# Weight gradient on one core: whole result stores, halved first loads, and another order of visits

## The chip, the cores and the metric

The kernel runs on one core of a Trainium2 chip. The metric is the time of one execution on the device in microseconds (us); less is better. Five engines work side by side and meet only through semaphores: TensorE (PE in the profile; PEld is its loading of weights), VectorE (DVE), ScalarE (ACT), GpSimd (POOL) and SyncE (SP, which here only issues DMAs). A set of 16 DMA engines moves data between the chip's main memory (HBM) and the core's on-chip memory (SBUF). TensorE writes its results to PSUM, which has eight banks.

## The reference

```
batch, m, k, n = 16, 512, 1024, 768
input        float32 [16, 512, 1024]      # X
grad_output  float32 [16, 512,  768]      # G
grad_weight = einsum('bmk,bmn->kn', input, grad_output)     # float32 [1024, 768]
```

Batch and m are summed over together: the result is X^T G, with X of 8192 x 1024 and G of 8192 x 768. The inputs are read once (58.7 MB), the result of 3.1 MB is written once.

## The kernel before

**Slices and pairs.** The 8192 rows are cut into 64 slices of 128 rows, and two slices make a load `u` from 0 to 31 (line 12, `LOADS`). Loads 0 to 3 and 31 are multiplied directly, slice by slice (kind `s`). Loads 4 to 30 are pairs (kind `P`): there the kernel uses a seven-product scheme for 2 x 2 blocks. The two slices of a pair and the two halves of X's and G's columns form the blocks, and sums and differences of blocks (`xe`, `ge`, made on VectorE by `sum_x` and `sum_g`, lines 193 to 211, three instructions each) let seven products do what eight would.

**Streams, blocks, visits.** Products are named by letters and digits. A, B, C and D are the four quarters of the result (A: left half of X's columns with the left half of G's; B: left with right; C: right with left; D: right with right); 1, 5, 6 and 7 are the products of pairs that more than one quarter needs. Each stream has four blocks, `q` = 0 to 3, of 128 x 384 numbers. One visit multiplies one slice, or one product of a pair, into one block: a weight load of 128 x 128 and a matmul over 384 columns. There are 916 visits. A block's partial sum stands in a PSUM bank while it is open; it is closed into SBUF (`acc` for A to D, `macc` for 1, 5, 6, 7) and opened again later, so that the eight banks serve 32 blocks.

**The order.** `PLAN` (line 15) is a string of tokens that a search outside the kernel has found; the loop at line 396 turns each into instructions, in this order on every engine. `C0@6.1` is one visit of block C0, opened in bank 6; `C0.2` two more visits. `cC0` closes a block by a copy on ACT, `vC0` by a copy or an addition on VectorE. `fC0@4` fills bank 4 with the block's sum again (ACT). `zcD1.22` sets a sum aside into a buffer of its own (ACT; `zv` on VectorE), and `yD1.22` adds it back (VectorE). `wC1` adds a shared product into a block on POOL. `x1.9` and `g1.9` are the steps that make the sums of pair 9. `r11` is one of twelve roundings of slices 0 and 1 from float32 to bf16 (lines 218 to 231). A visit can begin when its data has landed (and been summed or rounded), and when its bank has been closed and, if wanted, filled.

**Loads.** Slices 0 and 1 of X and slice 0 of G come as float32 through SP and ACT (lines 143 to 146), four DMAs in all. Everything else comes through POOL, which casts to bf16 on the way (lines 162 to 180): from load 3 on one DMA of 384 KB for G and one of 512 KB for X of each pair. POOL issues a load when a buffer and a place in its queue are free; ten pairs can be held.

**The end.** The last close of A to D adds the shared product, and `store` (lines 333 to 341) sends the block to HBM through SP. Its first six DMAs are halves of 64 rows (`HALVED = 3` blocks, line 99); the later ones are whole blocks of 128 rows and 192 KB. The last block, B3, lies in two banks (`fB3@3+4`): its 256-column part is copied by ACT and stored through ACT, its 128-column part by VectorE and SP.

Of the kernel before, what the change touches and what calls it, by code (L numbers as in the profile page):

```python
# [9 lines left out]
P = 128  # L10
# [5 lines left out]
    "r11 r10 r16 r15 r14 r13 C0@6.1 r12 C1@4.1 vC0 C2@7.1 A0.1 cC1 A2.1 C3@5.1 cC2 r0 A1.1 A3.1 cC3 D3@4.1 "  # L16
    "B3@6.1 r4 r1 B2@3.1 B1@7.1 r2 r3 D1@5.1 vD3 D1.1 A3.1 A2.1 cD1 B3.1 B2.1 B1.1 B0@4.1 cB2 B0.1 vB1 A1.1 "
    "cB3 D2@5.2 vB0 fC3@3 C0@7.1 A0.1 C2@6.1 cD2 C2.1 D0@4.2 vC2 D0.1 D2@5.1 C3.1 B2@6.1 vD2 A3.1 cC3 C0.1 "
    "A2.1 vD0 D1@5.1 B1@3.1 A0.2 C0.1 D1.1 A3.1 vC0 A1.1 zcD1.22 A1.1 C1@4.1 vB2 C1.2 C3@5.2 D3@6.4 C1.1 A3.1 "
    "vD3 A1.1 B1.2 vC3 B0@6.3 D0@7.2 vB0 D2@5.3 C1.1 B1.1 vD2 D3@6.1 A1.1 D0.1 vD3 A3.1 B2@5.2 vB1 B2.1 "  # L20
    "D1@6.2 vB2 C2@3.3 yD1.22 A0.2 vC2 C0@5.2 A2.2 vD1 A2.1 B3@3.1 vC1 B3.3 vC0 B3.2 A3.1 D0.1 vB3 D0.1 "
    "D3@5.2 vD0 fB1@3 B0@6.3 vD3 A2.2 vB0 D1@7.1 fC2@5 D1.1 D2@4.2 fC1@6 A0.2 vD2 B1.2 C1.1 g0.4 fC3@4 C1.1 "
    "A1.2 vD1 cB1 C2.2 g1.4 A3.1 C0@7.1 C3.1 g2.4 C3.3 x0.4 C3.1 C1.1 A2.1 cC3 C2.1 x1.4 C0.2 cC2 13@4.1 x2.4 "
    "B2@3.1 cC1 A3.1 vC0 A0.1 c13 B1@5.1 61@6.1 B2.1 vB1 B2.1 c61 B0@4.1 A1.1 vB2 B3@5.1 12@7.1 71@6.1 vB3 "
    "10@3.1 g0.5 11@5.1 vB0 11.1 x0.5 10.1 12.1 c11 13@4.1 A3.1 c12 A1.1 v13 50@5.1 c10 50.1 71.1 x1.5 A0.1 "
    "c50 73@7.1 g1.5 73.1 c71 g0.6 A2.1 51@3.1 c73 51.1 g2.5 61@4.1 53@5.1 c51 53.1 v61 60@7.2 c53 70@6.1 "
    "g1.6 70.1 fC0@4 52@3.1 g2.6 52.1 72@5.1 x2.5 72.1 c52 C0.1 x0.6 C0.1 A2.1 63@3.1 cC0 63.1 x1.6 70.1 72.1 "
    "73@4.1 c70 x2.6 60.1 A3.1 c72 v73 63.1 B0@6.1 c60 B0.1 g0.7 B3@5.2 fC1@7 B2@4.1 vB0 B2.1 A1.1 c63 A0.1 "
    "vB3 C1.1 62@6.2 g1.7 62.1 vB2 C2@5.2 c62 C1.1 g2.7 13@3.1 f51@4 13.1 x0.7 A1.1 C1.1 fC0@6 A2.1 v13 51.1 "
    "cC1 51.1 C2.1 x1.7 A3.1 c51 C0.1 vC2 11@3.2 cC0 A0.1 71@7.1 v11 fC3@4 71.1 53@6.2 f50@5 g0.8 C3.2 f52@3 "  # L30
    "v53 C3.1 50.2 g1.8 52.2 x2.7 12@6.2 g2.8 x0.8 12.1 A2.1 A3.1 zc12.3 A1.1 C3.1 x1.8 52.1 50.1 cC3 71.1 "
    "x2.8 73@6.1 c52 73.1 v71 72@4.1 c50 72.1 61@3.1 v73 61.1 fB1@5 61.1 v72 A0.1 63@6.1 fB2@7 63.1 v61 B1.2 "
    "f10@4 B1.1 v63 B1.1 B2.2 cB1 g0.9 10.2 f60@6 10.1 x0.9 10.1 B0@3.1 cB2 B0.1 A0.1 g1.9 c10 51@5.1 x1.9 "
    "51.1 f62@7 60.1 g2.9 60.2 x2.9 C2@4.2 c60 v51 62.3 y12.3 B3@6.2 c62 B3.1 vC2 A1.1 f53@5 B0.1 A3.1 vB3 "
    "70@7.1 f13@4 70.2 g0.10 zcB0.0 11@6.2 13.1 g1.10 f52@3 13.2 x0.10 11.1 A1.1 c13 A3.1 52.1 x1.10 52.1 "
    "fC1@4 53.1 g2.10 53.1 c52 53.1 v11 70.1 A2.1 c53 A2.1 x2.10 A0.1 f73@3 C0@6.1 v70 C0.2 fB2@5 C1.1 g0.11 "
    "C1.1 fC3@7 C1.1 73.1 vC0 73.1 cC1 B2.1 yB0.0 B2.1 f71@6 C3.2 72@4.1 x0.11 71.1 cC3 A3.1 A1.1 cB2 71.1 "
    "x1.11 71.1 f63@7 73.1 g1.11 72.2 c71 x2.11 61@5.2 v72 c73 61.1 63.2 g2.11 63.1 fB0@4 B1@3.1 v61 B1.1 "
    "f60@6 B1.1 g0.12 B0.2 c63 A2.1 vB1 51@5.1 cB0 51.1 60.1 g1.12 60.1 12@7.2 g2.12 c60 12.1 x0.12 12.1 "
    "fB3@3 A1.1 C2@6.2 fC1@4 v12 C2.1 51.1 B3.1 x1.12 f53@7 B3.1 C1.1 v51 A2.1 cB3 A0.1 53.1 g0.13 53.1 f50@3 "  # L40
    "C1.1 52@5.1 vC2 52.1 cC1 50.1 x2.12 50.2 f13@4 v52 50.1 C3@6.1 c53 C3.1 g1.13 A3.1 A0.1 fC0@5 vC3 13.2 "
    "c50 13.1 x0.13 11@7.2 f72@3 11.1 70@6.1 g2.13 70.1 v11 70.1 C0.2 x1.13 C0.1 72.1 g0.14 72.1 cC0 62@7.2 "
    "c72 v70 62.2 fB2@5 A0.1 x2.13 A2.1 63@3.1 c13 v62 63.1 A1.1 B2.1 g1.14 B2.1 fC2@7 B2.1 v63 10@4.2 cB2 "
    "10.1 x0.14 10.2 A0.1 51@6.1 x1.14 51.1 71@3.1 g2.14 71.1 zc51.23 71.1 v10 C2.2 61@5.1 v71 61.1 cC2 61.1 "
    "x2.14 A2.1 fB0@6 72@3.1 v61 73@4.2 fB3@7 73.1 g0.15 B0.1 f13@5 B0.2 v73 A1.1 A3.1 cB0 A3.1 v72 B3.3 13.1 "
    "x0.15 13.1 cB3 11@4.2 c13 g1.15 52@6.2 v11 52.1 53@7.2 v52 53.1 f60@4 B1@3.2 x1.15 B1.1 fC1@6 60.1 v53 "
    "60.1 f12@5 60.2 g2.15 A3.1 vB1 C1.1 c60 C1.2 fC3@7 g0.16 A0.1 70@4.1 A2.1 f50@3 12.1 g1.16 12.2 x0.16 "
    "12.1 50.2 c12 x2.15 50.2 cC1 g2.16 C3.2 v70 c50 C3.2 10@6.1 x1.16 10.1 cC3 A0.1 g0.17 A2.1 70@5.1 fC0@7 "
    "70.1 v10 A1.2 f71@3 A3.1 g1.17 62@6.1 v70 62.2 71.1 g2.17 71.1 C0.1 v62 C0.1 c71 C0.2 x0.17 A3.1 f61@3 "
    "A1.1 A2.1 cC0 C2@6.1 x1.17 C2.2 f73@5 x2.16 61.2 vC2 61.1 73.2 c61 x2.17 73.1 63@6.1 fB2@7 g0.18 63.3 "  # L50
    "fB1@3 y51.23 B0@4.2 c73 B0.1 g1.18 A0.1 B1.1 vB0 f72@5 B1.2 B2.1 g2.18 B2.1 cB1 B2.1 x0.18 B2.1 A0.1 "
    "A3.1 cB2 v63 51@4.3 x1.18 51.1 f63@6 72.2 x2.18 72.2 v51 52@3.3 g0.19 53@7.1 fB3@4 53.2 v52 63.1 B3.2 "
    "v53 c63 B3.2 g1.19 C1@3.2 cB3 C1.1 13@6.1 x0.19 13.1 f71@4 13.2 c72 A1.2 v13 71.3 vC1 f10@6 12@7.2 x1.19 "
    "12.1 f11@5 60@3.2 g0.20 c71 60.2 v12 11.3 v60 11.1 A0.1 A3.1 g1.20 70@7.1 f50@3 70.1 g2.19 70.1 g2.20 "
    "10.3 x0.20 10.1 50.2 c10 v70 50.2 A0.1 fB2@6 x2.19 A2.3 x1.20 c50 73@7.2 c11 x2.20 73.1 62@4.1 g0.21 "
    "fC3@3 62.3 B2.1 g1.21 B2.1 v73 B2.1 B1@5.2 cB2 v62 B1.1 C3.2 g2.21 C3.2 x0.21 C3.1 C2@7.2 cC3 C2.1 vB1 "
    "C2.1 A2.1 72@6.1 vC2 72.2 52@4.1 x1.21 52.2 g0.22 A3.2 61@3.1 v72 61.2 g1.22 61.1 51@7.2 v61 63@6.3 "
    "g2.22 f13@3 C0@5.1 v52 C0.3 v51 C0.1 fC1@4 13.2 x0.22 13.1 C1.2 c13 C1.1 x1.22 C1.1 zc63.13 A1.3 x2.21 "
    "fB0@6 x2.22 A0.2 B3@7.1 g0.23 cC1 B3.2 vC0 B3.1 51@3.2 vB3 B0.3 v51 B0.2 12@5.1 g1.23 12.1 cB0 12.1 "
    "x0.23 12.1 f72@7 A3.2 v12 A0.1 70@4.2 y63.13 70.2 A1.1 x1.23 72.2 v70 71@5.2 c72 71.1 g0.24 71.1 f10@6 "  # L60
    "53@3.2 g2.23 53.2 v71 53.1 A2.2 x2.23 11@4.1 v53 11.3 x0.24 11.1 A2.1 A3.1 50@5.2 x1.24 50.2 g1.24 "
    "62@7.1 v11 62.1 zc50.5 62.2 g0.25 51@3.1 f60@4 51.1 73@5.2 v51 73.2 60.1 g1.25 f61@3 60.1 v62 60.3 v73 "
    "61.1 fC2@7 61.2 c60 A0.1 x0.25 A0.1 10.1 fB2@5 10.2 x1.25 10.2 g2.25 63@4.2 c10 x2.24 63.2 x2.25 B2.2 "
    "g0.26 B2.3 v63 B1@6.2 cB2 B1.1 g1.26 B1.2 g2.26 B0@5.2 g2.24 B0.1 C3@4.1 vB1 C3.3 vB0 C3.1 C0@6.1 y50.5 "
    "C0.1 f52@5 C0.2 vC3 C2.1 c61 C2.2 x0.26 C2.2 60@4.1 A2.1 cC2 A2.1 x1.26 A3.1 f13@3 A3.1 x2.26 52.2 g0.27 "
    "52.3 v60 B3@7.2 c52 B3.1 vC0 B3.1 13.1 f52@4 13.1 g1.27 13.1 fB2@6 13.1 x0.27 13.1 12@5.2 c13 12.1 x1.27 "
    "12.1 52.1 73@3.1 v12 73.1 c52 73.1 A0.1 x2.27 A0.1 53@4.1 vB3 53.3 g0.28 50@5.2 v53 50.1 B2.2 g1.28 "
    "51@7.2 cB2 v50 A1.4 v51 A3.2 x0.28 f63@7 72@4.3 g2.28 72.2 x1.28 73.1 63.2 v73 63.1 70@6.2 g0.29 c63 "
    "70.2 fC3@3 g2.27 70.1 71@5.1 v72 71.1 f61@7 71.2 x2.28 71.1 C0@4.1 v70 C0.1 61.2 g1.29 61.2 vC0 C1@6.2 "
    "c61 g2.29 C1.2 x0.29 C1.1 f62@7 C1.2 C3.1 v71 C3.2 A1.1 x1.29 A1.1 cC3 62.1 vC1 62.3 g0.30 f71@6 62.1 "  # L70
    "11@3.1 x2.29 11.1 f12@5 11.1 g1.30 11.1 f10@4 11.1 A2.3 12.2 x0.30 12.1 10.2 c12 10.1 g2.30 10.2 x1.30 "
    "f61@5 11.1 71.1 c10 71.1 v11 62.1 61.2 f51@4 v62 13@3.3 v61 f60@7 51.2 x2.30 51.1 f72@5 51.1 60.1 v13 "
    "60.2 v71 60.2 72.2 v51 f63@6 wC1 A3.3 f73@3 A3.1 63.2 v60 A0.3 v72 fC1@7 A0.2 73.1 v63 f52@5 73.1 wC2 "
    "C1.2 fD1@4 v73 C1.1 52.2 cC1 52.1 A2.1 f53@6 A2.1 v52 A2.1 A1.1 f70@3 A1.2 fB2@7 D1.2 vA2 wD2 70.1 fC0@5 "
    "70.1 B2.2 v70 B2.3 vD1 fB1@3 C0.2 vA1 C0.1 fC2@4 C0.1 53.2 vC0 53.1 C2.2 vA3 fC3@5 C2.2 v53 C2.1 f50@2 "
    "C2.1 C3.2 cC2 C3.1 B1.2 vC3 fD3@6 wB3 B1.3 vA0 fB0@5 B1.2 vB2 50.1 fD2@4 50.2 vB1 D3.1 fD0@7 D3.1 D2.1 "
    "v50 D2.1 B0.2 cD2 B0.3 fB3@3+4 vD3 B0.2 D0.2 vB0 B3.4 vD0 B3.2 cB3 "
).split()


WARMUP = [("b", 512), ("f", 512), ("f", 512), ("b", 512)]
PAIRS_HELD = 10
SUMS_HELD = 8
ASIDE = 24

# [8 lines left out]
    2: [(1, 256, 0, 256), (2, 0, 256, 384)],  # L94
    3: [(2, 128, 0, 384)],
}


HALVED = 3


@with_exitstack
def kernel(
# [6 lines left out]
    nc = tc.nc  # L110
# [161 lines left out]
    stored = []  # L272
# [179 lines left out]
```

## Time and profile before

| | us |
|---|---|
| median of 3 runs (163.1 to 163.17) | 163.13 |
| the profiled execution's own time | 161.59 |
| its span, first to last instruction | 159.8 |
| TensorE busy | 154.8 (97% of the span) |
| VectorE busy | 143.7 (90%) |
| ScalarE busy | 96.4 (60%) |
| first matmul on data | 5.28 |
| last matmul ends | 155.86 |

The profile is one execution, and times in it count from its first instruction. The rows of the busy view have 40 slices of 4 us, each digit the busy share in tenths. A row of the timeline or of the chain begins with start and length in us; a bracket at its end tells how long the engine stood idle before and what ended that. `L323 MATMUL` are the visits, `L322` weight loads that are issued a second time, `L341` the stores. In the rows of the DMA issues the last number is the median time from issue to landing. Durations of neighbouring instructions of one engine overlap: VectorE's 128 x 384 additions take 551 ns each and start 468 ns apart when nothing waits.

### The profile page before, as it was taken

The page shows a single profiled execution, that of the slowest core. Times are in us where ns is not written, and L with a number is a line of the kernel's source. Part 1 is how long each engine was busy: PE and PEld are TensorE (multiplying, and loading weights), DVE is VectorE, ACT ScalarE, POOL GpSimd, SP SyncE. Part 2 cuts the span into 40 slices and gives each one's busy share as a digit, 9 for nine tenths or more (in the row PEclk, how much of TensorE's full clock was granted, in tenths as well). Part 3 has the DMA queues.
Part 4 walks back from the last instruction along what each step waited for, and adds up shares of the span by engine and source line. Part 5 has one row for each costly group of instructions (what it writes and reads, how often), then busy time and mean ns, then how long its engine had stood idle before and what let it go on. Part 6 is the DMA issues. An engine that isn't in the chain of part 4 may idle for free.

```text
span 159.8 us, 2985 instructions
## 1 busy us (share of the span) xinstructions
PE 154.8 (97%) x1002; PEld 99.1 (62%) x1129; DVE 143.7 (90%) x333; ACT 96.4 (60%) x219; POOL 39.7 (25%) x75
## 2 busy tenths in 40 slices
PE   8999999999999999999999999999999999999990
PEld 3466666567677777776665656666656666666560
DVE  0665989999999999999999999999999999898990
ACT  3761036588698999767868655254354525678750
POOL 7445222122221222221222221222222100024300
PEclk9999999999999999999999999999999999999998
DMA  5999999999999999999999999999999999931696
GB/s 176 298 209 212 216 212 212 213 213 215 210 212 213 213 214 212 213 213 215 213 213 214 212 214 211 213 215 209 214 214 213 215 211 214 212 73 28 172 366 226
DMA packets 12734, 33.41 MB, mean 209 GB/s; under 512 B 1456, under 2 KB 4528, under 8 KB 12720
## 3 DMA queue, kind: packets, MB, share of 16 engines
q0 software_dynamic: 9648, 28.64, 90.8%
q1 hardware_dynamic: 2640, 3.41, 6.7%
q10 hardware_dynamic: 432, 1.18, 1.9%
q8 instruction: 8, 0.13, 0.3%
q14 instruction: 6, 0.05, 0.1%
HBM read 58.72 MB, written 3.15 MB: 387 GB/s over the span
## 4 chain that ended last, share of the span: by engine, by line
PE 93%; DMA 3%; DVE 1%; ACT 0%; issue 0%; ACTq 0%
PE bank L323 93%; DMA xf<-in_input_dram 3%; DVE acc L366 1%; ACT xp L215 0%; ACT acc L362 0%; ACTq L362 0%
## 5 line engine op out<-in xcount | busy, mean ns | idle before, releaser
L323 PE MATMUL bank<-gp,xp 128*128 128x384 bf16 (+2 forms) x672 | 108.2, 307 | 0.3 <-DVE acc L366 0.2
L323 PEld LDWEIGHTS <-xp 128*128 128x128 bf16 x672 | 62.4, 97 | 31.4 <-DVE xp L215 1.7
L323 PE MATMUL bank<-ge,xe 128*128 128x384 bf16 x324 | 63.6, 326 | 0.0
L323 PEld LDWEIGHTS <-xe 128*128 128x128 bf16 x324 | 30.9, 97 | 15.4 <-DVE xe L197 0.4
L366 DVE TENSOR_TENSOR macc<-bank,macc 128x384 f32<-128x384 f32 x70 | 37.5, 551 | 0.6 <-PE bank L323 0.4
L362 ACT COPY macc<-bank 128x384 f32<-128x384 f32 x58 | 26.7, 482 | 13.5 <-PE bank L323 13.1
L294 ACT COPY bank<-macc 128x384 f32<-128x384 f32 x54 | 25.6, 484 | 9.0 <-DVE macc L366 5.7
L362 ACT COPY acc<-bank 128x384 f32<-128x384 f32 (+1 forms) x47 | 21.9, 477 | 14.6 <-PE bank L323 14.5
L294 ACT COPY bank<-acc 128x384 f32<-128x384 f32 (+1 forms) x48 | 22.6, 483 | 13.3 <-DVE acc L366 9.5
L366 DVE TENSOR_TENSOR acc<-bank,acc 128x384 f32<-128x384 f32 x51 | 26.8, 552 | 3.5 <-PE bank L323 2.9
L169 POOL DMA_DIRECT2D xp<-in_input_dram x29 | 15.3, 528 | 49.5 <-DMA xp<-in_input_dram 14.9
L168 POOL DMA_DIRECT2D gp<-in_grad_output_dram x29 | 15.3, 528 | 37.6 <-PE bank L323 20.4
L197 DVE TENSOR_TENSOR xe<-xp 128x1024 bf16<-128x1024 bf16 x27 | 18.5, 684 | 0.7 <-DMA xp<-in_input_dram 0.6
L207 DVE TENSOR_TENSOR ge<-gp 128x768 bf16<-128x768 bf16 x27 | 14.8, 550 | 0.0
L199 DVE TENSOR_TENSOR xe<-xe,xp 128x512 bf16<-128x512 bf16 x27 | 11.3, 420 | 0.4
L201 DVE TENSOR_TENSOR xp<-xp,xe 128x512 bf16<-128x512 bf16 x27 | 11.1, 419 | 0.2
L322 PEld LDWEIGHTS <-xp 128*128 128x128 bf16 x79 | 7.7, 98 | 4.6 <-DMA xp<-in_input_dram 0.4
L209 DVE TENSOR_TENSOR ge<-gp,ge 128x384 bf16<-128x384 bf16 x27 | 9.4, 350 | 0.1
L211 DVE TENSOR_TENSOR gp<-ge,gp 128x384 bf16<-128x384 bf16 x27 | 9.3, 351 | 0.1
L394 POOL TENSOR_TENSOR acc<-acc,macc 128x384 f32<-128x384 f32 x4 | 4.0, 1000 | 21.8 <-DVE macc L359 17.8
L378 ACT COPY aside<-bank 128x384 f32<-128x384 f32 x6 | 2.9, 480 | 6.0 <-PE bank L323 6.0
L322 PEld LDWEIGHTS <-xe 128*128 128x128 bf16 x48 | 4.7, 98 | 2.8 <-DVE xe L197 0.2
(23 smaller groups left out, 37.9 us busy)
## 6 DMA issues: line engine op xcount, KB each, us to landing
xp<-in_input_dram POOLq DMA_DIRECT2D x29, 512.0 KB, 16.8
gp<-in_grad_output_dram POOLq DMA_DIRECT2D x29, 384.0 KB, 16.8
out_dram<-acc SPq DMA_DIRECT2D x12, 192.0 KB, 2.2
xf<-in_input_dram ACTq DMA_DIRECT2D x2, 512.0 KB, 5.0
xp<-in_input_dram POOLq DMA_DIRECT2D x4, 256.0 KB, 8.5
gp<-in_grad_output_dram POOLq DMA_DIRECT2D x5, 192.0 KB, 7.7
out_dram<-acc SPq DMA_DIRECT2D x6, 96.0 KB, 2.2
gf<-in_grad_output_dram SPq DMA_DIRECT2D x2, 192.0 KB, 4.1
```

The source lines that it names most:

```text
L168: nc.gpsimd.dma_start(out=gp, in_=G[rows, :].rearrange("(p m) n -> p m n", m=2))
L169: nc.gpsimd.dma_start(out=xp, in_=X[rows, :].rearrange("(p m) k -> p m k", m=2))
L197: nc.vector.tensor_sub(out=xe[:, 0:2, :], in0=x[:, 1::-1, :], in1=x[:, 3::-2, :])
L199: nc.vector.tensor_sub(out=xe[:, 2, :], in0=xe[:, 0, :], in1=x[:, 0, :])
L201: nc.vector.tensor_add(out=x[:, 1, :], in0=x[:, 2, :], in1=xe[:, 2, :])
L207: nc.vector.tensor_add(out=ge[:, 0:2, :], in0=g[:, 0:2, :], in1=g[:, 1::2, :])
L209: nc.vector.tensor_add(out=ge[:, 2, :], in0=g[:, 3, :], in1=ge[:, 0, :])
L294: copy(out=tile_[:, t0 : t0 + c1 - c0], in_=sum_of(p, q)[:, c0:c1])
L322: nc.tensor.ldweights(stat)
L323: nc.tensor.matmul(tile_[:, t0 : t0 + c1 - c0], stat, mov[:, c0:c1], start=start, stop=True, skip_group_check=True,)
L362: nc.scalar.copy(out=d, in_=b)
L366: nc.vector.tensor_add(out=d, in0=b, in1=d)
```

## The change

Three things are changed. All result blocks are stored whole. X of slice 0 and G of slice 0 (each half of its columns) are loaded in two halves of 64 rows, in the same queues as before. And `PLAN` is replaced by another order that the search has found, for the same 916 visits.

```diff
-HALVED = 3
...
-    nc.sync.dma_start(out=gf[:, LEFT], in_=G[0:P, LEFT])
-    nc.scalar.dma_start(out=xf[0], in_=X[0:P, :])
-    nc.sync.dma_start(out=gf[:, RIGHT], in_=G[0:P, RIGHT])
+    HALVES = (slice(0, P // 2), slice(P // 2, P))
+    for rows in HALVES:
+        nc.sync.dma_start(out=gf[rows, LEFT], in_=G[0:P, LEFT][rows, :])
+        nc.scalar.dma_start(out=xf[0][rows, :], in_=X[0:P, :][rows, :])
+    for rows in HALVES:
+        nc.sync.dma_start(out=gf[rows, RIGHT], in_=G[0:P, RIGHT][rows, :])
     nc.scalar.dma_start(out=xf[1], in_=X[P : 2 * P, :])
...
-        halves = [slice(0, P)]
-        if len(stored) < 2 * HALVED:
-            halves = [slice(0, P // 2), slice(P // 2, P)]
-        for rows in halves:
-            stored.append(rows)
-            queue.dma_start(out=OUT[rows, row, at : at + c1 - c0], in_=sum_of(p, q)[rows, c0:c1])
+        queue.dma_start(out=OUT[:, row, at : at + c1 - c0], in_=sum_of(p, q)[:, c0:c1])
```

The order of visits, its beginning and its end:

```diff
-    "r11 r10 r16 r15 r14 r13 C0@6.1 r12 C1@4.1 vC0 C2@7.1 A0.1 cC1 A2.1 C3@5.1 cC2 r0 A1.1 A3.1 cC3 D3@4.1 "
-    "B3@6.1 r4 r1 B2@3.1 B1@7.1 r2 r3 D1@5.1 vD3 D1.1 A3.1 A2.1 cD1 B3.1 B2.1 B1.1 B0@4.1 cB2 B0.1 vB1 A1.1 "
+    "r11 r10 r16 r15 r12 r13 C0@4.1 r14 C3@3.1 r0 C2@5.1 A2.1 cC3 A1.1 vC2 A0.1 cC0 A3.1 D1@7.1 D0@6.1 B2@3.1 "
+    "D2@5.1 r4 r2 B1@4.1 vD1 cD0 B1.1 A0.1 r3 A3.1 vB1 B0@6.1 cD2 B0.1 B3@7.1 r1 B3.1 cB0 B2.1 A1.1 C1@4.1 "
...
-    "C2.1 C3.2 cC2 C3.1 B1.2 vC3 fD3@6 wB3 B1.3 vA0 fB0@5 B1.2 vB2 50.1 fD2@4 50.2 vB1 D3.1 fD0@7 D3.1 D2.1 "
-    "v50 D2.1 B0.2 cD2 B0.3 fB3@3+4 vD3 B0.2 D0.2 vB0 B3.4 vD0 B3.2 cB3 "
+    "cC1 wD2 B1.1 C0.1 vA2 C0.1 fB2@4 C0.3 vB1 fC2@6 50.2 fD2@7 vC0 50.1 B2.2 f53@5 v50 B2.2 fD3@3 D2.2 53.2 "
+    "cD2 vB2 53.1 D3.2 v53 C2.1 fC3@4 C2.2 fB0@7 C2.3 vA3 fD0@5 C2.1 wB3 C3.2 vD3 C3.1 D0.2 vC3 B0.3 vD0 "
+    "fB3@3+4 B0.2 vC2 B0.2 B3.2 vB0 B3.4 cB3 "
```

Counted over both strings: visits 916 and 916, fills 102 and 103, closes on ACT 105 and 102, closes on VectorE 150 and 144, sums set aside and added back 6 and 12, additions on POOL 4 and 3.

## The prediction

> **What bounds the kernel now.** I read the page's busy rows first, then the chain that ended last, then TensorE's weight loads for the waits behind it, then the stages of the DMA.
>
> ```profile
> PE   8999999999999999999999999999999999999990
> DVE  0665989999999999999999999999999999898990
> DMA  5999999999999999999999999999999999931696
> ```
>
> Three resources are full at once: TensorE, VectorE (90% of the span) and, until slice 35, the DMA engines. The chain says where one hands over to another:
>
> ```profile
> 0.73 4.12 DMA xf<-in_input_dram
> ...
> 5.29 22.56 PE bank L323 x153
> 27.85 0.02 issue
> 27.87 1.55 DVE acc L366 x3
> 29.42 0.04 issue
> 29.46 13.38 PE bank L323 x85
> 42.84 0.06 issue
> 42.90 112.86 PE bank L323 x746
> ```
>
> Columns are start, length, work. Work on data starts at 5.29 us, when X of slice 0 has landed (4.86) and been rounded; the last matmul ends at 155.86. The orders hold 916 visits; one visit is 384 columns and starts 162.5 ns after the one before it where nothing waits, so 149 us of the 150.6 are streaming, and gaps between matmul starts add to 1.3 us: 13 gaps, of which 1.13 us lie before 42.9 us and 0.19 us (four gaps) after. An order of visits can win at most those. The gaps before 42.9 end on loads:
>
> ```profile
> 20.66 1.41 PEld L323 LDWEIGHTS <-xp 128*128 128x128 bf16 x10 [0.26 <-DMA xp<-in_input_dram]
> ...
> 29.78 0.44 PEld L323 LDWEIGHTS <-xp 128*128 128x128 bf16 x4 [0.71 <-DMA xp<-in_input_dram]
> ...
> 42.85 0.10 PEld L322 LDWEIGHTS <-xp 128*128 128x128 bf16 x1 [0.40 <-DMA xp<-in_input_dram]
> ```
>
> Here TensorE stands still until X of pairs 3, 5 and 8 has landed (20.62, 29.74, 42.81). After that it stays 0.1 to 0.6 us behind nearly every landing. So the landing of pair 8 fixes the time of all that follows, and what shifts the load stream shifts the end. The stream itself, by stage (us, then busy time and count of each engine, clock, DMA share, GB/s):
>
> ```profile
> 1.75:2.75 1.00, 1.00 (x2) 0.33 (x1) 0.00 (x0) 1.00 (x1) 1.00 (x3) 1.00 0.89 204
> 2.75:4.25 1.50, 1.50 (x3) 0.48 (x2) 0.00 (x0) 0.19 (x1) 1.50 (x4) 1.00 0.99 395
> ...
> 43.00:139.00 96.00, 96.00 (x634) 63.38 (x736) 94.19 (x221) 61.66 (x141) 20.59 (x39) 1.00 1.07 213
> ...
> 149.00:151.00 2.00, 2.00 (x15) 1.21 (x13) 2.00 (x6) 1.54 (x4) 0.16 (x1) 1.00 0.66 158
> 152.00:156.00 4.00, 3.85 (x30) 2.50 (x28) 3.86 (x10) 2.13 (x6) 0.00 (x0) 1.00 1.02 367
> ```
>
> The engines fill up within a second microsecond and never go idle again until 139 us (213 GB/s counts the bf16 that lands; twice that is read). The last two rows are stores: in halves of 64 rows 158 GB/s, whole 367.
>
> **Part 1: three blocks stored whole instead of in halves.** Lines 333 to 341 no longer split the first three blocks: 17 stores in all where there were 20 (one of them ACT's in both). What it costs now:
>
> ```profile
> 148.97 1.80 SPq L341 DMA_DIRECT2D out_dram<-acc  x3
> ...
> 155.80 0.91 SPq L341 DMA_DIRECT2D out_dram<-acc  x2
> ...
> out_dram<-acc SPq DMA_DIRECT2D x4, 96.0 KB, 2.2
> ...
> out_dram<-acc SPq DMA_DIRECT2D x1, 64.0 KB, 2.6
> ```
>
> The first row is two halves and one whole store, 0.60 us each; later ones follow every 0.49 us. The halves put SP 0.87 us behind (the fourth block, A1, is closed at 149.37 and issued at 150.24); the queue stays full to 154, and a whole store needs 0.53 us of the engines (196.6 KB by 367 GB/s), so the arrears pass from SP to the engines: a store lands 2.05 us after its issue at 151.3 but 2.58 after it at 156.3. That last one lands at 158.90, and 0.91 us of closing work ends the span at 159.81. Without halves SP saves three issues of 0.6 us, all in the first 4 us of the tail, where nothing waits for it; what reaches the end is the arrears, at most 0.5 us.
>
> **Part 2: the end of the order.** The last 18 visits change. Before, VectorE closes D3, B0 and D0 from 154.27 to 155.75, and B3's two parts follow: SP is still busy with D0 until 156.21, so B3's narrow part, copied by 156.18, is issued at 156.32. After, D0 closes before C2 and B0; B0's last visit is 6 visits (0.98 us) before the end, so VectorE has closed it some 0.3 us before TensorE is done and SP is free. B3 now gets four visits in one step, so its wide part is complete four 128-column matmuls (0.21 us) before the end instead of two (0.11): ACT copies 0.1 us earlier. Counting back from the end, the last six blocks become ready 2.9, 2.4, 1.9, 1.4, 0.7 and 0.3 us before it, mean spacing 0.53, the engines' own pace, with a pause of 1.4 us ahead of them. Arrears go. The last issue moves from 0.45 to 0.35 us after the last matmul and its landing from 2.58 to 2.1 to 2.4. Parts 1 and 2 together: a gain of 0.2 to 0.6 us; I take **0.45**. The cover of ACT's store (issued 0.37 us after the last matmul, landing 2.50 later) moves the same way.
>
> **Part 3: slice 0 in halves.** SP issues four loads for two, ACT three for two; ACT's table load (1.66 us, 1.28 long) moves back by one issue of 0.41 and still ends a microsecond before the first rounding at 4.38. SP has nothing queued behind until the stores. A rounding now waits for two landings; the first half's is the earlier and costs nothing. X of slice 1 is issued 0.41 us later; its packets have no turn before 4.2 us anyway. What decides is how fast 64 rows load. The trace has no such load. Nearest row: stores of 64 rows, packets of the same 1536 bytes. From 147.5 to 151 us 406 packets took 59.9% of 16 engines, from 151 to 154.5 us 903 took 100.4%: 83 ns against 62, and with the 4-byte ones out (80 and 102) about 101 against 69. A half is not a whole at half length: each packet is slower.
>
> Bounds for the stream: at the good end, the half issue of G costs 0.19 us instead of 0.38 ahead of X, whose first packet follows G's by 0.38 us now: 0.2 us earlier. At the bad end halves with the same rows are always in flight together and go at half rate: of the 721 KB of X and G's left half, 204 pass in the slow first microsecond as now, and the other 517 need 2.5 us at 205 GB/s instead of 1.26: 1.2 us later. Between: G's packets run 0.38 us ahead, so its second half rides beside X's first. Then X alone sets the time, 524 KB at about 210, 2.5 us, with 197 KB of G beside it: 721 KB that full rate would pass in 1.76. Of the 0.74 lost, some 0.3 fall into the slow start that is there anyway. I take **0.4 us** later, since both queues start as now and alternate packet by packet. G of slice 1 and all pairs follow by as much, TensorE waits for them at pairs 5 and 8, and the end moves by all of it.
>
> In the Trainium skill, "SBUF — State Buffer", section "Door 1: The DMA port swizzle", 64 neighbouring partitions reach only 8 of 16 ports; the 158 against 367 GB/s agree. By its half rate alone the sum would be the bad end.
>
> **Part 4: the order of visits.** First uses of loads barely move: pair 5 at visit 146 in both, pair 8 at 224 in both, pair 14 at 384 instead of 385, pair 30 at 812 instead of 811. At the old landings no first use after pair 5 would come too early, so the order neither adds a load wait nor can win one. G of slice 1 is needed at visit 12 instead of 13: 0.16 us more waiting there, swallowed by the waits at pairs 5 and 8. VectorE's work: 111 adding closes for 121, but 12 sums set aside and added back for 6 (549 ns each), and 9 copies for 6: with one more final close and one sum set aside by VectorE itself that is one instruction more, 0.47 us of its 144. It is full from 30 us on; by visits its account differs from before's by 0 to 0.5 us either way (beyond a constant 0.47 from the first 16 visits, where it was idle). What of its backlog reaches TensorE was 0.19 us after 42.9; the bounds are 0 and some 0.7 (the gap of 0.33 at 28.98, when it closed three blocks in a row, twice over). I take 0.19 again: nothing.
>
> **Sum.** 0.4 later, 0.45 earlier, 0: minus 0.05 us on the profiled execution's 161.59 (span 159.8 and 1.8 around it). That execution is 1.5 us under the median of the three runs; the difference carries over: 163.13 - 0.05, **163.1 us**. Below 0.2% (0.33 us) a measurement here can't tell a change from none: I forecast no change.
>
> **Rivals.**
> *Halves load as fast as wholes.* Reads that wait for memory may hide the slower packets; the first row of stages (204 GB/s) shows engines waiting then. Against it, the stores. No cost, or 0.2 gained, less 0.45: 163.13 - 0.55, **162.6**. The Trainium skill's "Perfetto Trace Analysis", "DMA Optimizations", says smaller chunks may let some start sooner where engines are idle; no run here shows it.
> *Halves in step* (slower): X's and G's first halves go together, then the second halves, at the bad end of part 3. For it, alternating queues; against it, G's head start. The page on SBUF named above would have it so. 163.13 + 1.2 - 0.45, **163.9**. It decides from a delay of 0.8 us on.
> *VectorE late.* With no idle time between 30 and 140 us, a crowded stretch of closes holds banks back: 0.7 us after pair 8, **163.75**. For it, visits 820 to 880, where the new order asks 10.45 us of VectorE in 9.75; against it, 900 visits on which the accounts match.
> *The stores gain nothing,* since the last waits for its own close anyway: **163.5**. Against it, the growing landings.
>
> **Chances.** Forecast 0.36 (its own range 162.8 to 163.45), fast halves 0.28, in step 0.17, VectorE late 0.14, stores 0.05. Faster 0.28, same 0.36, slower 0.36. Range 162.4 (early start and the full 0.6) to 164.0 (in step with the smaller gain); below and above it I leave a tenth each.
>
> **What would show it.** Right: X of pair 8 lands 0.4 us after 42.81, the first matmul comes 0.05 to 0.5 us after 5.29, the last store lands 2.1 to 2.4 us after its issue, the span less the last matmul's end is 3.4 to 3.5 instead of 3.95, and gaps after pair 8 are near 0.2 us. Wrong: a first matmul before 5.2, pair 8 at or before 42.8, or VectorE releasing gaps of over 0.5 us late in the run.

## The result and the profile after

The change takes 167.2 us (median of 4 runs, 166.64 to 168.39) where the kernel before takes 163.12 beside it: a ratio of 1.028, interval 1.021 to 1.035. It is 4 us slower; forecast was no change, 163.1, in a range of 162.4 to 164.0.

The profiled execution of the change took 167.31 us, its span 165.5 (before 161.59 and 159.8). The busy view, 40 slices of 4.14 us:

```profile
PE   8199999999999999999999999999999999999991
...
DVE  0135698999999999999999999999999999889991
...
PEclk9957999999999999999999999999999999999999
DMA  4999999999999999999999999999999999300775
```

What differs lies in the first slices. TensorE stands nearly idle in the second, and its granted clock falls to 5 tenths and 7 tenths in the third and fourth; from the fifth on its row reads as before, VectorE's from the sixth, but for the shift at the end. The timeline of the change up to the first visit (start, length, what; the bracket is idle time and what ended it):

```profile
0.73 1.18 SPq L143 DMA_DIRECT2D gf<-in_grad_output_dram  x2
0.74 1.45 ACTq L144 DMA_DIRECT2D xf<-in_input_dram  x2
...
6.98 1.28 ACT L216 ACT_TABLE_LOAD   x1 [6.98 <-DMA gf<-in_grad_output_dram]
...
8.67 7.54 PE L323 MATMUL bank<-gp,xp 128*128 128x384 bf16 x30 [3.79 <-ACT gp L216]
```

The first visit begins at 8.67 us instead of 5.28. The chain that ended last says what it waited for. From there on TensorE runs to the end with hardly a break: the two closes on ACT at 39.9 us make one matmul start 0.29 us late.

```profile
1.33 5.57 DMA gf<-in_grad_output_dram
...
6.98 0.25 ACT L216
7.23 1.04 issue
8.27 0.36 ACT gp L216
...
8.67 31.20 PE bank L323 x191
39.87 0.02 issue
39.90 0.38 ACT macc L357
40.27 0.04 issue
40.31 0.49 ACT acc L357
40.80 0.04 issue
40.84 120.99 PE bank L323 x798
```

The second half of G's left part, issued at 1.33, lands at 6.91; only then does ACT load its table (1.28 us) and round. The DMA issues of the change, with KB each and the median us from issue to landing, stand against 5.0 us for X and 4.1 for G before:

```profile
xf<-in_input_dram ACTq DMA_DIRECT2D x2, 256.0 KB, 4.9
xf<-in_input_dram ACTq DMA_DIRECT2D x1, 512.0 KB, 8.1
gf<-in_grad_output_dram SPq DMA_DIRECT2D x4, 96.0 KB, 6.3
```

In the median, half the bytes take about as long or longer, and the whole load behind them (X of slice 1) takes 8.1. Single landings, from the trace:

| lands at, us | before | change (first, second half) |
|---|---|---|
| G of slice 0, left | 4.35 | 3.22, 6.91 |
| X of slice 0 | 4.86 | 4.60, 7.19 |
| G of slice 0, right | 5.67 | 9.06, 10.48 |
| X of slice 1 | 7.14 | 10.31 |
| G of slice 1 (POOL's first) | 7.49 | 7.14 |

One load became earlier: POOL's. The stages of the change (us, busy time and count of each engine, granted clock, DMA share, GB/s):

```profile
1.75:2.75 1.00, 1.00 (x2) 0.33 (x1) 0.00 (x0) 0.00 (x0) 1.00 (x3) 1.00 0.89 197
2.75:4.25 1.50, 1.50 (x3) 0.48 (x2) 0.00 (x0) 0.00 (x0) 1.50 (x4) 1.00 0.84 196
4.25:5.25 1.00, 0.64 (x2) 0.00 (x0) 0.00 (x0) 0.00 (x0) 1.00 (x3) 1.00 1.17 319
...
8.67:14.75 6.08, 6.08 (x22) 2.75 (x22) 2.27 (x6) 3.29 (x9) 2.61 (x5) 0.51 1.13 221
14.75:20.00 5.25, 5.25 (x40) 3.50 (x39) 3.82 (x8) 1.09 (x3) 2.05 (x5) 1.00 1.11 215
```

and two rows of the same view of the kernel before:

```profile
4.25:5.25 1.00, 0.95 (x2) 0.00 (x0) 0.66 (x3) 0.72 (x3) 1.00 (x3) 1.00 1.07 419
...
8.67:14.75 6.08, 6.08 (x42) 3.77 (x41) 3.74 (x8) 2.48 (x6) 3.00 (x6) 1.00 1.13 207
```

From 2.75 to 4.25 us the change moves 196 GB/s where 395 moved before. And from 8.67 to 14.75 TensorE is "busy" all the time in both, but does 22 matmuls against 42, at a clock of 0.51. A full busy row is not full speed; the count beside it shows that. Matmuls are not quite visits: 80 of the 916 visits go to a block that lies across two banks, and such a visit is two matmuls, over 256 and over 128 columns.

**Where the 5.7 us of span come from.** By 14.75 us the change has begun 20 visits and the kernel before 57 (counted in the trace's records, a split visit once). 37 visits of 0.1625 us are 6.0 us, and the last matmul ends 5.96 us later (161.81 against 155.85). So the whole loss has been made by 14.75 us; behind it the late starts of matmuls add to about 1 us in both kernels. The end gives 0.28 back: the span less the last matmul's end is 3.69 instead of 3.96.

### The profile page after: what moved, and what is told of

It is laid out like the page before. It is cut to its first block, busy times and chain, and to the rows that moved or that the text cites. A ratio compares the mean times of both kernels' runs of the same rounds, so it can differ in the third digit from the quotient of the medians.

```text
span 165.5 us, 3000 instructions
## 1 busy us (share of the span) xinstructions
PE 157.1 (95%) x1002; PEld 100.4 (61%) x1129; DVE 143.5 (87%) x334; ACT 97.0 (59%) x222; POOL 39.0 (24%) x74
## 4 chain that ended last, share of the span: by engine, by line
PE 92%; DMA 3%; ACT 1%; issue 1%; SPq 0%; DVE 0%; ACTq 0%
PE bank L323 92%; DMA gf<-in_grad_output_dram 3%; SPq L143 0%; ACT acc L357 0%; ACT macc L357 0%; ACT gp L216 0%; DVE acc L359 0%; ACT L216 0%; ACTq L216 0%
## 5 line engine op out<-in xcount | busy, mean ns | idle before, releaser
L323 PE MATMUL bank<-gp,xp 128*128 128x384 bf16 (+2 forms) x672 | 110.9, 312 | 3.8 <-ACT gp L216 3.8
L323 PEld LDWEIGHTS <-xp 128*128 128x128 bf16 x672 | 63.6, 99 | 36.1 <-DVE xp L216 3.8
L323 PEld LDWEIGHTS <-xe 128*128 128x128 bf16 x324 | 31.1, 97 | 15.2 <-DVE xe L198 0.8
L357 ACT COPY macc<-bank 128x384 f32<-128x384 f32 x66 | 30.2, 481 | 16.4 <-PE bank L323 14.8
L294 ACT COPY bank<-macc 128x384 f32<-128x384 f32 x64 | 30.1, 484 | 9.3 <-DVE macc L361 5.0
L361 DVE TENSOR_TENSOR acc<-bank,acc 128x384 f32<-128x384 f32 x57 | 30.4, 553 | 3.4 <-PE bank L323 2.5
L361 DVE TENSOR_TENSOR macc<-bank,macc 128x384 f32<-128x384 f32 x54 | 29.4, 552 | 1.4 <-PE bank L323 1.0
L294 ACT COPY bank<-acc 128x384 f32<-128x384 f32 (+1 forms) x39 | 18.5, 483 | 20.3 <-DVE acc L361 17.3
L357 ACT COPY acc<-bank 128x384 f32<-128x384 f32 (+1 forms) x36 | 16.9, 477 | 11.0 <-PE bank L323 10.5
L322 PEld LDWEIGHTS <-xp 128*128 128x128 bf16 x77 | 7.5, 98 | 4.7 <-DVE xp L202 0.2
L354 DVE TENSOR_TENSOR acc<-bank,macc 128x384 f32<-128x384 f32 (+2 forms) x15 | 6.8, 496 | 0.0
```

What stands on the lines that cost most here:

```text
L294: copy(out=tile_[:, t0 : t0 + c1 - c0], in_=sum_of(p, q)[:, c0:c1])
L323: nc.tensor.matmul(tile_[:, t0 : t0 + c1 - c0], stat, mov[:, c0:c1], start=start, stop=True, skip_group_check=True,)
L357: nc.scalar.copy(out=d, in_=b)
L361: nc.vector.tensor_add(out=d, in0=b, in1=d)
```

## The experiments

**Which part of the change costs?** E1 puts only the halved loads into the kernel before; E2 is the change with the four whole loads back; E3 is the kernel before with whole stores alone.

```diff
 E3
-HALVED = 3
+HALVED = 0
```

> The kernel before with nothing changed but the loads of slice 0, which come in halves of 64 rows as in the changed kernel; order and stores are the old ones. Theory 1 (the halved loads make the loss: the first matmul comes at 8.7 us instead of 5.3, then TensorE runs at half clock for 6 us): first matmul at 8 to 9 us, clock 0.5 behind it, 3.5 to 5 us slower, 166.5 to 168. Theory 2 (the new order makes the loss, because it was made for other landings): within 1 us of 163.1.

> The changed kernel with whole loads of slice 0 again; new order and whole stores stay. Theory 1: first matmul at 5.3 us, and what is left is the tail of the prediction, 0.2 to 0.6 us faster than before: 162.5 to 163.0. Theory 2: still 3 us or more slower, 166 to 167.

> The kernel before with whole stores alone. If the arrears of the first six half stores reach the end, as predicted, the last store lands 2.2 to 2.4 us after its issue instead of 2.58 and the time falls by 0.1 to 0.4 us. If the last store waits for its own close anyway, the same within 0.1 us.

E1: 167.67 us (166.36 to 168.72), ratio 1.032 (1.027 to 1.038). E2: 162.49, 0.9997 (0.997 to 1.002). E3: 161.83, 0.9976 (0.995 to 1.0004). The halved loads hold the whole loss; order of visits and stores together are neutral to 0.3%. In E1 the first matmul comes at 7.48 us, sooner than the 8 to 9 expected, but TensorE then works in two batches and at half clock from 8.8 to 15.6 us:

```profile
7.48 1.51 PE L326 MATMUL bank<-gp,xp 128*128 128x384 bf16 x10 [2.28 <-DVE xp L218]
11.04 1.46 PE L326 MATMUL bank<-gp,xp 128*128 128x384 bf16 x4 [2.05 <-ACT xp L218]
```

The ten matmuls of the first batch (eight visits) need only slice 0 and G's left part; the next wait for X of slice 1 (landed 10.25) and its rounding. E3 can't be told from no change by its interval, because executions of this kernel fall in two groups. 23 runs of before beside it: ten from 161.72 to 162.05 (mean 161.94), thirteen from 162.77 to 163.24 (162.97). E3: seven with mean 161.65 and five with 162.74. Within each group whole stores are 0.23 to 0.29 us shorter. E2 falls in the same way, three runs with mean 161.72 and nine with 162.54, 0.22 and 0.43 shorter. E3's profiled execution is of the upper group and shows what may set it: X of pair 3 lands at 22.08 instead of 20.62, and TensorE stands 1.55 us. Its last store lands 2.19 us after its issue (2.2 to 2.4 were expected).

**Is it the table load?** E4 lets ACT copy one column right after its load issues.

```diff
+    tiny = accp.tile([P, 1], f32, name="tiny")
+    nc.scalar.copy(out=tiny, in_=nc.const_aps.tensor(1.0, (P, 1), f32))
```

> The changed kernel with one more instruction on ACT, a copy of one column, right behind its load issues, so that the table load no longer stands behind the wait for the second half of G. Theory 1 in its parts: the table load (1.28 us) moves from 6.98 to about 2.8 us, the first matmul from 8.67 to about 7.4, the time falls by 1 to 1.5 us. Rival: X and its rounding or the clock set the pace there, and the time falls by less than 0.4 us.

167.55 us (165.81 to 167.93), 1.030: no gain. The timeline of E4:

```profile
2.86 1.28 ACT L150 ACT_TABLE_LOAD   x1 [2.86 <-issue]
...
7.45 1.48 PE L326 MATMUL bank<-gp,xp 128*128 128x384 bf16 x9 [2.25 <-DVE xp L219]
11.49 1.78 PE L326 MATMUL bank<-gp,xp 128*128 128x384 bf16 x5 [2.56 <-DVE gp L219]
```

The table is in early and the first visit comes 1.2 us sooner than in the change, but after nine matmuls (seven visits) TensorE stands again until G's right part is there (10.98). What the first batch wins, the second's landings take back, and the clock is at half from 8.46 to 15.29 us all the same. This is why a wait on the chain need not be worth its length.

**Is it the clock?** E5 and E15 are the change with three more warm-up matmuls, which keep TensorE busy to about 8 us; E16 is the change again.

```diff
-WARMUP = [("b", 512), ("f", 512), ("f", 512), ("b", 512)]
+WARMUP = [("b", 512), ("f", 512), ("f", 512), ("f", 512), ("f", 512), ("f", 512), ("b", 512)]
```

> The changed kernel with three more warm-up matmuls on constants (about 0.9 us each), so that TensorE has work until about 7.6 us while slice 0 is awaited. If the half clock behind the first matmul (0.53 granted from 10 to 15 us) comes from that idle time and is lost time, the clock stays at 1.0, the 13 visits after the landing of G's right half at 10.5 us save 0.16 us each, and the time falls by 1.5 to 2.5 us, to about 165. Rival: the loads set the pace up to 15 us and the half clock is hidden behind them: less than 0.4 us.

> The change with three warm-up matmuls more, again, beside the change itself. Theory (the half clock costs some 1.5 us in the executions that show it): clock above 0.99 in all, 165.5 to 166, 1 to 1.5 us under the change's mean. Rival (the clock is not part of it, the two kernels spread alike): within 0.5 us of the change's mean.

> The change itself, unaltered. Theory: 166.6 to 168.4 again; the executions at a mean clock of 0.977 have the half clock from the first visits to some 14.7 us, and those near 1.0 have none and are late because G's right half and X of slice 1 land later still (over 11 us). Rival: executions near 1.0 have the same landings as the profiled one, so the clock costs nothing.

E5: 165.73 (two runs), 1.022 (1.013 to 1.031). E15: 165.61 (164.98 to 166.33), 1.022 (1.018 to 1.026). E16: 167.67 (166.46 to 169.18), 1.033 (1.028 to 1.037). E15's six runs have a mean of 165.68, E16's without its longest, 167.44: 1.8 us. The stage row of E5:

```profile
8.67:14.75 6.08, 5.06 (x34) 2.92 (x34) 3.64 (x9) 4.09 (x11) 2.61 (x5) 1.00 1.13 223
```

E5 lands its loads no sooner (second batch at 11.07), but works at full clock: 34 matmuls in the stage against 22 of the change. By 14.75 us it has begun 30 visits instead of 20, worth 10 x 0.1625 = 1.6 us, and its last matmul ends 1.7 us sooner (160.10). So a longer warm-up wins back 1.5 to 1.8 us of the loss without a byte landing sooner. E16's profiled execution was its longest, 169.18 us: X of slice 1 and G's right part land at 11.49 and 11.84, and the clock is at half from 6.92 to 17.16 us, longer than in the first profile. One thing stays open. Of ten executions of the change two have a mean clock of 1.0 and still take 168.4; they weren't profiled, so the second half of E16's expectation, what makes them long, is not settled.

**More loads, or 64 rows, or POOL?** The packet records of the trace show an order of events. In the change SP's queue moves G's first half from 2.0 to 2.75 us and then almost nothing until 4.25; ACT's queue is dry from about 3.75 to 4.5. POOL's first packets come at 3.31, inside that hole, 132 of them by 5.0 us. Before, neither queue had a hole and POOL's packets began at 5.24. From 6.5 to about 9 us the three queues mostly get 10 to 15 packets each per quarter of a microsecond, so that SP and ACT crawl. That the holes let POOL in is read from this order of events; what POOL's packets cost is tested by holding them back. E6 makes as many loads, but of 128 rows and half the columns. E7 keeps the halves and holds POOL back with four memsets (its first issue at 2.95 instead of 1.24); E12 does both.

```diff
 E6, E12 (G's left and right part, X likewise)
+    nc.sync.dma_start(out=gf[:, 0:192], in_=G[0:P, 0:192])
+    nc.scalar.dma_start(out=xf[0][:, 0:KH], in_=X[0:P, 0:KH])
+    nc.sync.dma_start(out=gf[:, 192:NH], in_=G[0:P, 192:NH])
...
 E7, E12
+    scratch = accp.tile([P, 512], f32, name="scratch")
+    for _ in range(4):
+        nc.gpsimd.memset(scratch, 0.0)
```

> The changed kernel with slice 0 cut into as many DMAs, but by columns: each has 128 rows and half the bytes per row. Theory A (the number of DMAs does it: each half is short, the queue runs dry before the next one's first packet, and POOL's loads step in): POOL's first packets at 3.3 us as in the changed kernel, first matmul after 8 us, 166 or more. Theory B (the 64 rows do it): first matmul before 5.8 us, POOL's packets after 4.8 us, time 162 to 163.5.

> The changed kernel with four fills of a spare buffer on POOL ahead of its first load, so that POOL's loads are issued some 2 us later. If the second halves are late because POOL's packets take the engines from 3.3 us on, they land at 5.2 to 6 us instead of 6.9 and 7.2, G's right half and X of slice 1 by 8 instead of 10.4, and the time falls by 2 us or more. If the second halves are late by themselves (their descriptors come late), they land at 6.5 or later still and the time does not fall by more than 0.5 us, as the loads of the pairs are later too.

> Whole rows, cut by columns into as many loads as the change has, and POOL's first load held back to about 3 us by four memsets. If POOL's packets, which step in when the two queues are dry for a moment, are what delays the third and fourth load: G's right half and X of slice 1 land before 7.2, one batch of visits from 5.4 on with no wait over 0.5 us, clock 1.00, 163 to 163.7. Rival (a third load in a queue comes late by itself, however its rows lie and whoever else loads): G's right half at 7.5 or later, TensorE waits over 1.5 us in 6 to 10, 165 or more.

E6: 167.15 us, 1.031 (1.019 to 1.042), two runs. E7: 164.75, 1.016 (1.007 to 1.024), two runs. E12: 164.04, 1.014 (1.005 to 1.023), with runs far apart. PE timelines of E6, E7 and E12:

```profile
5.41 1.59 PE L323 MATMUL bank<-gp,xp 128*128 128x384 bf16 x9 [0.21 <-DVE xp L216]
10.29 2.10 PE L323 MATMUL bank<-gp,xp 128*128 128x384 bf16 x6 [3.28 <-DVE gp L216]
```

```profile
6.79 1.83 PE L327 MATMUL bank<-gp,xp 128*128 128x384 bf16 x9 [1.95 <-ACT gp L220]
9.19 3.07 PE L327 MATMUL bank<-gp,xp 128*128 128x384 bf16 x12 [0.57 <-DVE gp L220]
```

```profile
5.41 1.93 PE L327 MATMUL bank<-gp,xp 128*128 128x384 bf16 x9 [0.20 <-DVE xp L220]
7.86 4.41 PE L327 MATMUL bank<-gp,xp 128*128 128x384 bf16 x30 [0.52 <-DVE gp L220]
```

With whole rows (E6) the first batch is on time, since X and G's left part land by 5.04; but the third and fourth load of SP come nearly as late as in the change (G's right part 8.05 and 9.77, against 9.06 and 10.48). SP's queue is dry from 4.25 to 4.75 us and ACT's nearly dry from 4.5 to 5.25, POOL's packets begin at 4.04, TensorE idles 3.28 us, and its clock is 0.56 in the stage up to 14.75 and at half until 16.25. So more and shorter loads do nearly all of the damage without a single load of 64 rows. With POOL held back the same loads (E12) land by 7.34 and TensorE hardly waits in the profile. E7 stands between: POOL is out until 6.69 us, yet X lands at 6.26 and G's right part at 8.68 (up to 6 and 8 were expected); 2.4 us of the time come back. E7's stages show the rate of 64 rows, E12's that of 128, both without POOL:

```profile
2.75:4.25 1.50, 1.50 (x3) 0.49 (x2) 0.00 (x0) 0.00 (x0) 1.50 (x4) 1.00 0.99 279
4.25:5.25 1.00, 0.58 (x2) 0.00 (x0) 0.13 (x1) 0.16 (x1) 1.00 (x3) 1.00 0.96 202
```

```profile
2.75:4.25 1.50, 1.50 (x3) 0.48 (x2) 0.26 (x1) 0.67 (x1) 1.50 (x4) 1.00 1.03 337
4.25:5.25 1.00, 0.96 (x2) 0.00 (x0) 0.19 (x1) 0.55 (x2) 1.00 (x3) 1.00 1.05 377
```

The engines are as busy at 202 GB/s as at 377. In profiled spans E7 is 162.9, E12 160.6. In times the gap is less sure: E12's runs were 162.3 and 163.0, about the kernel before, and 165.0 and 165.4 at a mean clock of 0.987. Only the first was profiled, so E12 shows that holding POOL back can undo nearly all of the loss, not that it always does.

**Do the remedies add?** E13 is the change with table, warm-up and memsets; E14 is E12 with the longer warm-up.

> The change with all three remedies: the table load right after ACT's issues, POOL's loads held back, three warm-up matmuls more. Theory (one chain: the landings set the two batches, the table load and the warm-up lie beside them): first visits near 6.8, second batch near 9.2 as with POOL held back alone, clock at 1.00, so at most 0.7 us under that run's 164.75: 164.0 to 164.6. Rival (the remedies add, 2.4 for POOL, 1.5 for the clock, 1.3 for the table): 162 to 162.5.

> By columns, POOL held back, three warm-up matmuls more: against the run with three remedies (164.05, ratio 1.011) only the cut differs, 128 rows by half the columns instead of 64 rows. Theory (a load of 64 rows passes at half rate): the second batch starts near 7.9 instead of 9.44, the ratio is 1.000 to 1.006. Rival (rows or columns, the cut costs the same once POOL is held back and the clock is full): second batch near 9.4, 1.009 to 1.013.

E13: 164.05 us (163.9 to 164.16), 1.011 (1.006 to 1.016): they don't add; they are one chain, whose second batch starts at 9.44. E14: 163.94, 1.010 (1.006 to 1.015), on the rival's side, but not for the rival's reason. The end of its warm-up and its first visits:

```profile
8.26 0.38 PE L156 MATMUL bank<-const-bfloat16-1.0 128*128 128x512 bf16 x1
8.48 0.76 PE L327 MATMUL bank<-gp,xp 128*128 128x384 bf16 x4
```

The warm-up itself lasts past 8.26 us and is now the bound, while all loads of slice 0 have landed by 7.97 (8.93 in E13). The same warm-up ends a microsecond sooner in E13, because there the clock is granted in full from 4.69 us on and in E14 only from 6.80. So this pair doesn't price the rows, and what half rate costs in time beyond the profiled 2.3 us stays open.

**Which tensor?** E8 halves only G, E10 only X; E9 halves X on both queues at the same moment and leaves G whole.

```diff
 E8 (left part; the right part likewise; E10 the other way round)
+    nc.scalar.dma_start(out=xf[0], in_=X[0:P, :])
+    for rows in HALVES:
+        nc.sync.dma_start(out=gf[rows, LEFT], in_=G[0:P, LEFT][rows, :])
...
 E9
+    for rows, queue in zip(HALVES, (nc.sync, nc.scalar)):
+        queue.dma_start(out=xf[0][rows, :], in_=X[0:P, :][rows, :])
+    nc.sync.dma_start(out=gf[:, LEFT], in_=G[0:P, LEFT])
+    nc.sync.dma_start(out=gf[:, RIGHT], in_=G[0:P, RIGHT])
```

> Only G of slice 0 comes in halves; X is one load, issued first on ACT. Theory (each load of 64 rows runs at half rate, and every load behind one is late): X lands by about 5, G's left part near 6, its right part behind four issues of SP near 8.5; X of slice 1, now second on ACT, by 7.5. First visits near 6.5, a second wait for G's right half to about 9; 165 to 166 us. Rival (what costs is X, 524 KB of the 721; G's halves ride beside it for nothing): first visits before 5.7, no second wait, 163 to 163.5.

> Only X of slice 0 comes in halves, both on ACT; G is two whole loads on SP. Theory (half rate, and X of slice 1 late behind two halves): G's left part near 4.5, its right part near 6 to 7, X near 6.5, X of slice 1 near 9 to 10; first visits near 7, TensorE then has G's right half and waits later or not at all, 164.5 to 165.5. Rival (G's halves are what is late; X's cost nothing): X by 5.2, 163 to 163.5.

> The changed kernel with G of slice 0 whole and X of slice 0 in two halves of 64 rows, one on SP and one on ACT, issued at the same moment. Theory A (a queue that runs dry between two short DMAs): each queue still has one short DMA at its head, POOL's packets come in before 4.5 us and X lands after 6. Theory B (64 rows reach half the memory side, so halves hurt only one after the other): X lands by 5.2 us, first matmul by 5.7, time 162 to 163.5.

E8: 166.9 us, 1.029 (1.023 to 1.034), a microsecond over the theory's figure. E10: 165.87, 1.022 (1.016 to 1.027), just over its own. E9: 165.12, 1.018 (1.005 to 1.031), two runs, and fits neither of its theories. Halving either one is enough. In E8 X lands on time (4.38), but the second half of G's left part lands at 7.24, with the table load behind it, and the first visit is at 9.00. In E10 both of G's parts have landed by 4.85 and X's second half lands at 7.97. What my figures left out is the clock, 0.51 in E8's stage from 8.67 to 14.75 us and 0.75 in E10's. E9 has the halves of X side by side. They land at 4.55 and 5.62, the second later than the whole at 4.86, and G's right part lands only at 9.47. SP's queue is dry there from 3.75 to 4.25 us and POOL still begins only at 5.20, so a hole doesn't always let POOL in.

The same count as above, for some of the runs:

| | visits begun by 14.75 us | last matmul ends | span |
|---|---|---|---|
| before | 57 | 155.85 | 159.8 |
| E2, whole loads | 54 | 156.30 | 160.0 |
| E12, columns and POOL later | 50 | 156.88 | 160.6 |
| E13, three remedies | 40 | 158.45 | 162.1 |
| E7, POOL later | 36 | 159.18 | 162.9 |
| E5, longer warm-up | 30 | 160.10 | 163.8 |
| E1, halved loads alone | 20 | 162.22 | 166.4 |
| the change | 20 | 161.81 | 165.5 |

What a kernel is short of by 14.75 us, at 0.1625 us a visit, it is late by at its last matmul. This holds within 0.2 us in all profiles but four: in E1, E6 and E16 the clock stays at half beyond 14.75 us and the last matmul is 0.4 to 1.0 us later still, and E3 (57 visits) loses 1.3 us at pair 3. No version was faster than the kernel before by more than its interval.

## Why the prediction was wrong

**Part 3, the halves, is the step that failed.** It took 0.4 us, with bounds of -0.2 and 1.2; the last matmul came 5.96 us later. Three of its premises broke.

*"Both queues start as now and alternate packet by packet."* The first halves did start, but each queue then fell nearly dry between its loads, and POOL's loads, which have none of slice 0, went in (E6, E7, E12). I had priced how fast 64 rows pass, not whether the queue has packets to pass. The sentence on X of slice 1, "its packets have no turn before 4.2 us anyway", fell with it: it landed 3.2 us later.

*"G of slice 1 and all pairs follow by as much."* The stream was treated as one shift. In truth POOL's loads came earlier at first (7.14 against 7.49) and X of pair 8 0.9 us later (43.70 against 42.81), and none of TensorE's waits in the change ends on a pair's load. The end was set by the first visits, not by the stream that I followed. The stream also held TensorE less than I read: the 0.26, 0.71 and 0.40 us are idle times of its weight loads, and the matmuls behind them started only 0.04, 0.16 and 0.22 us late.

*TensorE's clock.* No term or rival had a price for TensorE idling. After 3.79 us of it the clock was 0.51 for six microseconds, and keeping TensorE busy instead won 1.5 to 1.8 us (E5, E15). In the Trainium skill, "TensorE: Matmul & The Clock Gate", section "What's actually happening", the half clock is the idle state, entered after an idle window of some 3.4 us. Idles of 3.79 and, in E8, 4.13 us agree. But the clock was halved too after idles of 1.95 us (E7), 2.25 (E4) and 2.28 (E1), while E9, with two of 1.84 and 1.93, kept 1.00: here idles well under that length were enough, and what decides among them no run shows.

*ACT's table load* was said to move by one issue and to end before the first rounding. It moved to 6.98 us, behind the landing of G's second half. So it does in every profile that has G in halves of 64 rows and no early copy on ACT (7.31 in E8); where G is whole or cut by columns it runs ahead of the wait (2.59 in E10, 2.14 in E6). That the first half's landing "costs nothing" was right for the rounding and wrong for what is queued in front of it. In time the error was nothing (E4).

**Parts 1 and 2, the tail, were right in direction, and the size was off.** 0.45 was taken, bounds 0.2 to 0.6; span less last matmul fell by 0.28, to 3.69 where 3.4 to 3.5 was the sign of being right, and E3's groups say 0.23 to 0.29. The last store's row of the change:

```profile
out_dram<-acc SPq DMA_DIRECT2D x1, 64.0 KB, 2.0
```

It lands 2.0 us after its issue (2.1 to 2.4 forecast, 2.6 before), and 2.39 instead of 3.05 after the last matmul: 0.66 won. But what follows the last landing grew from 0.91 to 1.30 us, where I had taken it as fixed. E3, with whole stores and the old order, ends 3.68 us after its last matmul as well, though its last store lands 2.60 us after it and the change's 2.39; all fifteen profiles with whole stores lie between 3.67 and 3.69. So the whole stores alone give the 0.28, and the new end of the order, part 2, adds nothing to it. What sets the 3.68 us is open.

**Part 4, the order: nothing, right.** E2, which has the new order and the whole stores, gives 0.9997, within its groups much what the stores alone give, and nothing in its profile waits long late in the run. No run has the new order alone, so a few tenths of a microsecond either way can't be excluded.

**The rivals.** "Halves in step" named a true mechanism, half rate (202 against 377 to 419 GB/s in the stage from 4.25 to 5.25 us), but its 1.2 us is a small part of the 6 us lost. In the Trainium skill, "SBUF — State Buffer", section "Door 1: The DMA port swizzle", 64 neighbouring partitions reach only half of the ports; the rates agree. "Halves load as fast as wholes" is wrong. In the Trainium skill, "Perfetto Trace Analysis", section "DMA Optimizations", smaller chunks may let some start sooner. That much came true, the first halves did land sooner (3.22 for 4.35), but G's right part was complete 4.8 us later (10.48 for 5.67). "VectorE late" and "the stores gain nothing" didn't come.

## What to carry to other kernels

Splitting a load does not only change when its bytes come: it adds a load to the queue, and when a queue runs dry between its loads, another queue's loads can go in and keep a share from then on. Ask of a first load what stands behind it in its own queue and what waits in others, and count the work done by a fixed time, since a busy row can be at half clock. Where TensorE must wait at the start, a warm-up that lasts to the first data is cheap cover; one that outlasts the data (E14) becomes the bound itself.

## What the hardware showed that I had not expected

- A load issued behind another in its queue starts late. In the change SP's first load was issued at 0.73 and had packets at 2.0; the second, issued at 1.33, had its bulk from 4.25 on. In E13, where POOL was out, SP's third load, issued at 1.96, began at 5.0. Why is open.
- Issuing takes longer where a queue has loads of 64 rows: 0.55 to 0.84 us each in the change, against 0.38 to 0.46 before. Whole loads behind them are slow to issue too (X of slice 1: 0.60 in the change, 0.83 in E9). By columns (E6) it takes 0.39 to 0.46, so it isn't the number of loads.
- The clock comes back late: in the change whole visits started 320 ns apart, instead of 162.5, from 8.67 to about 14.6 us, with TensorE busy nearly throughout. In the profiles where it fell early it stayed at half for 3.4, 6.8 or 10.2 us (E7, the change, E16).
